# Five blocks of the output projection moved into the last attention units, and the residual chains in another order

## The chip, the cores and the metric

The kernel runs on one core of a Trainium2 chip. TensorE (PE) does matmuls into PSUM, VectorE (DVE) and ScalarE (ACT) work on vectors, GpSimd (POOL) does little here, and SyncE (SP) issues most loads. The metric is the time of one execution on the device in microseconds; lower is better. 2829.44 us is the median of three runs of the kernel before.

## The reference

One transformer block on 1024 tokens of width 1024, with 256 context tokens, in fp32. A hybrid mixer (differential attention of 4 heads, and a short convolution of width 512) is projected by `w_out`; the result is normalised, gated and added to `x`; a router chooses 128 tokens for each of 16 experts.

```
out  = concat([attn, conv], -1) @ w_out            # the mixer's output projection
h    = x + G1 * rmsnorm(out)                        # G1: gate times gain, from the ada vector
xn2  = rmsnorm(h) * A2 + SH2                        # A2, SH2: scale and shift
aff  = softmax(xn2 @ w_router)                      # 16 experts
g, i = top_k(aff.T, 128)                            # for each expert its 128 tokens
y    = scatter(g * (silu(xn2[i] @ w_gate) * (xn2[i] @ w_up)) @ w_down)
```

## The kernel before

Each fp32 operand is split into a high part in fp32r (an ACT cast) and the rest (a DVE subtraction), and each product is three matmuls, hi*hi, hi*lo and lo*hi (`mm3`, with `split` at L87 and L88). A scheduler orders the instructions when the program is built; on the chip each engine works its own list in order, and so does each DMA queue.

**Attention** runs 32 units, four heads by eight blocks of 128 queries. A unit has its scores (`sc`, one unit ahead), the softmax (`probs`: the exponentials `e`, their sum and scaling on ACT and DVE, then ten transposes `tp` and their split into `a`), and, for every second unit, the products with V for two query blocks (`values`: 30 matmuls `av`, a norm, and a store of the columns to `mixT_d` in DRAM by POOL's queue). Between them the 18 convolution jobs, 24 matmuls each, are spread over the first `NCV` units. At the end of unit `NCV` - 1, `out_weights` loads w_out in eight pieces of 512 KB through two `raw` buffers and splits them into `woh` and `wol`, which stay in SBUF.

**Phase 2** then loads the rows `G1`, `SH2`, `A2` and the router weights `wr`, and sends `SH2` through the router once (`rb`). For each of eight token blocks, `mixed` loads the block's columns of `mixT_d` (`mraw`), splits them (`mh`, `ml`), and runs 2 x 24 matmuls `mm<-woh` and `mm<-wol` into two PSUM banks. Behind them stands the residual chain: squares on ACT (L608), `rstd`, two operations with `G1` on DVE (L613), the addition of `x` (L614), another square (L616), the product with `A2` (`xn`, L620), eight transposes of `xn` on PE (L640), their copies (L641), sixteen router matmuls `lg` (L644), and a softmax that ends with L631 on DVE. Two blocks together give 32 rows of `affT`. When all of `affT` is there, `choose` runs 16 rounds of MAX8 and its companions on DVE (L656 first), and the expert layers follow; the small `ple` projection stands on PE behind the last block's router matmuls. From the sixth block on, the loads of the first expert weights (`next_raw`) stand between the blocks.

## Time and profile before

| | |
|---|---|
| median of 3 runs | 2829.44 us (2826.55 to 2829.99) |
| the profiled execution | 2830.79 us, its span 2828.9 us |
| mean granted clock of TensorE | 0.97 |
| busy share of the span | PE 93%, DVE 71%, ACT 57%, POOL 9% |

The profile is of one execution; the span runs from its first instruction to its last, and the execution's own time is 1.9 us longer. Attention's last part, phase 2 and the start of the top-k rounds lie between 280 and 700 us of the span; the rest of the program is the projection before and the experts behind, which the change does not touch.

### The profile page before, as it was taken

How to read it: one execution, taken by the hardware profiler on the slowest of the kernel's cores; microseconds unless marked ns; L12 is line 12 of the kernel's file. 1: busy time of each engine (PE TensorE's matmuls, PEld its weight loads, DVE VectorE, ACT ScalarE, POOL GpSimd, SP SyncE). 2: the span in 40 equal slices, each digit the busy share in tenths (PEclk: the TensorE clock that was granted, in tenths of full speed). 3: DMA queues.
4: the chain of work that ended last, by engine and by line, in shares of the span. 5: the costliest groups of instructions: out<-in, count | busy, mean ns of one | idle time of the engine just before them, and what ended most of it. 6: DMA issues, size and time to landing. Idle time of an engine off the chain costs nothing.

```text
span 2828.9 us, 38725 instructions
## 1 busy us (share of the span) xinstructions
PE 2636.2 (93%) x14237; PEld 2216.2 (78%) x14237; DVE 1998.8 (71%) x3298; ACT 1620.6 (57%) x2858; POOL 250.1 (9%) x355
## 2 busy tenths in 40 slices
PE   8999999898799999997799999998999998989998
PEld 5777888787588877775689999997878787777786
DVE  6965899845698888885656767763777676785535
ACT  4213898734477777775644555543665665674335
POOL 0101000001300000000100000000111110231000
PEclk9999999999899999999799999999999999999999
DMA  7666332245699999997512122336665667465612
GB/s 302 203 236 211 90 96 90 91 160 198 241 390 381 363 377 370 375 359 239 218 39 46 46 46 38 49 79 171 168 168 136 161 156 144 143 186 200 195 60 82
DMA packets 306018, 516.44 MB, mean 183 GB/s; under 512 B 52529, under 2 KB 180094, under 8 KB 304804
## 3 DMA queue, kind: packets, MB, share of 16 engines
q1 hardware_dynamic: 288556, 456.04, 51.0%
q0 software_dynamic: 11136, 36.25, 4.3%
q10 hardware_dynamic: 6136, 21.67, 2.0%
q8 instruction: 113, 1.85, 0.3%
q14 instruction: 77, 0.63, 0.1%
HBM read 421.01 MB, written 92.88 MB: 182 GB/s over the span
## 4 chain that ended last, share of the span: by engine, by line
PE 72%; DMA 10%; ACT 7%; DVE 6%; issue 3%; SPq 1%; POOL 0%; DVEq 0%; ACTq 0%; POOLq 0%
PE mm L82 13%; PE mm L84 13%; PE mm L83 12%; PE av L1333 2%; PE pu L763 2%; PE pu L764 2%; PE pu L762 2%; PE pg L763 2%; PE py L764 2%; PE py L763 2%; PE py L762 2%; PE pg L764 2%; PE sc L1052 2%; PE pg L762 2%; PE tp L1324 1%
## 5 line engine op out<-in xcount | busy, mean ns | idle before, releaser
L88 DVE TENSOR_TENSOR wlo<-raw,whi 128x2048 fp32r<-128x2048 f32 (+1 forms) x280 | 541.9, 1962 | 172.2 <-ACT whi L87 168.1
L87 ACT CAST whi<-raw 128x2048 fp32r<-128x2048 f32 (+1 forms) x284 | 459.8, 1656 | 136.5 <-PE mm L83 62.1
L82 PE MATMUL mm<-uh,whi 128*128 128x512 f32 x640 | 257.4, 402 | 0.9 <-ACT uh L824 0.9
L83 PE MATMUL mm<-ul,whi 128*128 128x512 f32 x640 | 254.1, 397 | 0.0
L84 PE MATMUL mm<-uh,wlo 128*128 128x512 f32 x640 | 253.8, 397 | 0.0
L84 PE MATMUL mm<-whi,ul 128*128 128x256 f32 x768 | 220.9, 288 | 0.0
L82 PE MATMUL mm<-whi,uh 128*128 128x256 f32 x768 | 220.6, 287 | 0.0
L83 PE MATMUL mm<-wlo,uh 128*128 128x256 f32 x768 | 218.2, 284 | 0.0
L82 PEld LDWEIGHTS mm<-whi,uh 128*128 128x128 f32 x768 | 147.4, 192 | 0.2
L84 PEld LDWEIGHTS mm<-whi,ul 128*128 128x128 f32 x768 | 147.5, 192 | 0.1
L83 PEld LDWEIGHTS mm<-wlo,uh 128*128 128x128 f32 x768 | 147.2, 192 | 0.2
L1302 ACT ACTIVATE lg<-lg,sm 128x128 f32<-128x128 f32 (+7 forms) x128 | 99.5, 777 | 82.2 <-DVE sm L1301 81.6
L84 PEld LDWEIGHTS mm<-uh,wlo 128*128 128x128 f32 x640 | 122.3, 191 | 24.4
L446 ACT ACTIVATE e<-sc,mx 128x512 f32<-128x512 f32 (+1 forms) x192 | 117.9, 624 | 40.3 <-DVE mx L445 39.5
L82 PEld LDWEIGHTS mm<-uh,whi 128*128 128x128 f32 x640 | 122.2, 191 | 22.9 <-ACT uh L824 1.4
L83 PEld LDWEIGHTS mm<-ul,whi 128*128 128x128 f32 x640 | 122.4, 191 | 21.7
L82 PE MATMUL mm<-xh,whi 128*128 128x512 f32 x320 | 127.2, 399 | 2.4 <-DVE stl L88 1.4
L1333 PE MATMUL av<-pT,V 128*128 128x256 f32 x640 | 109.9, 300 | 19.6 <-ACT pT L87 13.8
L83 PE MATMUL mm<-xl,whi 128*128 128x512 f32 x320 | 126.9, 398 | 0.0
L84 PE MATMUL mm<-xh,wlo 128*128 128x512 f32 x320 | 126.3, 396 | 0.5 <-DVE wlo L88 0.5
L1333 PEld LDWEIGHTS av<-pT,V 128*128 128x128 f32 x640 | 92.3, 196 | 43.0 <-ACT pT L87 30.5
L1298 DVE SCALAR_TENSOR_TENSOR lg<-sc,FT,nF 128x512 f32<-128x512 f32 (+3 forms) x160 | 91.6, 582 | 39.7 <-PE sc L1295 27.1
(392 smaller groups left out, 7006.2 us busy)
## 6 DMA issues: line engine op xcount, KB each, us to landing
raw<-in_w_gate_dram SPq DMA_DIRECT2D x64, 1024.0 KB
raw<-in_w_up_dram SPq DMA_DIRECT2D x64, 1024.0 KB
raw<-in_w_down_dram SPq DMA_DIRECT2D x64, 1024.0 KB
raw<-in_w_in_dram SPq DMA_DIRECT2D x76, 512.0 KB
wada<-in_w_ada_dram SPq DMA_DIRECT2D x32, 512.0 KB
Q<-Q_d SPq DMA_DIRECT2D x64, 256.0 KB
yraw<-yT_d SPq DMA_DIRECT2D x22, 512.0 KB
wa<-in_w_ada_dram SPq DMA_DIRECT2D x8, 1024.0 KB
```

The lines of the kernel that those rows point to most:

```text
L82: self.nc.tensor.matmul(ps, ah, bh, start=(i == 0), stop=False)
L83: self.nc.tensor.matmul(ps, ah, bl, start=False, stop=False)
L84: self.nc.tensor.matmul(ps, al, bh, start=False, stop=(i == n - 1))
L87: self.nc.scalar.copy(hi, src)
L88: (eng or self.nc.vector).tensor_tensor(lo, src, f(hi), op=ALU.subtract)
L446: nc.scalar.activation(e[:, c0:c0 + n], ps[:, :n], AF.Exp, scale=-1.0, bias=mx[:, m, c:c + 1], accum_out=sm[:, m, c:c + 1])
L762: self.nc.tensor.matmul(ps[n], xh[:, i, :], hi[:, k, c], start=(i == 0), stop=False)
L763: self.nc.tensor.matmul(ps[n], xh[:, i, :], lo[:, k, c], start=False, stop=False)
L764: self.nc.tensor.matmul(ps[n], xl[:, i, :], hi[:, k, c], start=False, stop=(i == KB - 1))
L1298: nc.vector.scalar_tensor_tensor(lg[:, c0:c0 + full], ps[:, :full], Ft, nF[:, c0:c0 + full], op0=ALU.subtract, op1=ALU.add)
L1302: nc.scalar.activation(lg[:, :n], lg[:, :n], AF.Exp, scale=-1.0, bias=sm[:, 0:1], accum_out=sm[:, 1:2])
L1333: nc.tensor.matmul(ps[:, :256], V[:, k, :], pT[k // 4][j][:, k % 4, :], start=(k + j == 0), stop=(k == nkb - 1 and j == 1))
```

## The change

`NCV` falls from 31 to 27, so that the convolution ends and w_out is loaded four units sooner. In the units 28 to 31, ahead of `probs`, `out_early` does the whole output projection of token blocks 0 to 3, and behind the last `probs` that of block 4. It loads the block's columns of `mixT_d`, splits them, runs the two halves through one PSUM bank (`mm`, one buffer), copies each to SBUF (`cy`) on ACT, and stores the block to the new DRAM tensor `pre_d` on POOL's queue. Phase 2 loads `pre_d` back into three of the six buffers of the weight loads, and its blocks go in the order out(5), chain 0, chain 4, out(6), chain 1, chain 5, out(7), chains 2, 6, 3, 7, where only blocks 5, 6 and 7 have matmuls. `rb` is computed behind the matmuls of block 5.

```diff
--- before.py
+++ after.py
@@ -30,7 +30,8 @@
 CAP = 128
 SB = 1
 LOOK = 1
-NCV = 31
+NCV = 27
+EARLY = 5
 NR = 6
 PB = 4
 FPROJ = 104
@@ -81,7 +82,7 @@
         for i, ((ah, al), (bh, bl)) in enumerate(pairs):
             self.nc.tensor.matmul(ps, ah, bh, start=(i == 0), stop=False)
             self.nc.tensor.matmul(ps, ah, bl, start=False, stop=False)
-            self.nc.tensor.matmul(ps, al, bh, start=False, stop=(i == n - 1))
+            self.lastmm = self.nc.tensor.matmul(ps, al, bh, start=False, stop=(i == n - 1))
 
     def split(self, src, hi, lo, eng=None):
         self.nc.scalar.copy(hi, src)
@@ -116,6 +117,7 @@
         self.dr = self.pool(st, "dram", space=DRAM)
         dt = lambda n, s, d=F32: self.t(self.dr, s, d, n)
         self.mixT_d = dt("mixT_d", [D, SEQ])
+        self.pre_d = dt("pre_d", [EARLY * P, D])
         self.h_d = dt("h_d", [SEQ, D])
         self.K_d = dt("K_d", [HEADS, 2, P, KEYS])
         self.Q_d = dt("Q_d", [HEADS, 2, P, SEQ])
@@ -393,7 +395,11 @@
                 self.conv(*x, w, 1)
             if i + 1 == NCV:
                 self.out_weights(w)
+            if 0 <= i - n + EARLY - 1 < EARLY - 1:
+                self.out_early(i - n + EARLY - 1, w)
             self.probs(i, *E.pop(i))
+            if i + 1 == n:
+                self.out_early(EARLY - 1, w)
             if i % 2:
                 self.values(i)
 
@@ -411,6 +417,30 @@
                     r0 = kh * 512 + j * 256
                     nc.sync.dma_start(raw, self.I["w_out"][0, r0:r0 + 256, n * 512:(n + 1) * 512].rearrange("(k p) c -> p k c", p=P))
                     self.split(raw, hi[:, j * 2:j * 2 + 2, :], lo[:, j * 2:j * 2 + 2, :])
+
+    def out_early(self, tb, w):
+
+        nc = self.nc
+        part = self.out_lhs(w, tb, ("raw", "whi", "wlo"), (2, 2))
+        y = self.t(w, [P, SEQ], F32, "cy", bufs=1)
+        for n in range(2):
+            ps = self.t(self.pp, [P, 512], F32, "mm", bufs=1)
+            self.out_half(ps, part, n)
+            nc.scalar.copy(y[:, n * 512:(n + 1) * 512], ps)
+        self.store(self.pre_d[tb * P:(tb + 1) * P, :], y)
+
+    def out_lhs(self, w, tb, tags, bufs):
+        raw = self.t(w, [P, KB, P], F32, tags[0], bufs=bufs[0])
+        self.nc.sync.dma_start(raw, self.mixT_d[:, tb * P:(tb + 1) * P].rearrange("(k p) t -> p k t", p=P))
+        mh = self.t(w, [P, KB, P], F32R, tags[1], bufs=bufs[1])
+        ml = self.t(w, [P, KB, P], F32R, tags[2], bufs=bufs[1])
+        self.split(raw, mh, ml)
+        return mh, ml
+
+    def out_half(self, ps, part, n):
+        mh, ml = part
+        wo = self.wo
+        self.mm3(ps, [((mh[:, k, :], ml[:, k, :]), (wo[n, k // 4][0][:, k % 4, :], wo[n, k // 4][1][:, k % 4, :])) for k in range(KB)])
 
     def scores(self, i):
         nc, w, pp = self.nc, self.wp, self.pp
@@ -547,15 +577,19 @@
         with ExitStack() as st:
             w = self.pool(st, "p2")
             pp = self.pool(st, "p2p", 2, space=PSUM)
-            wo = self.wo
             G1, SH2, A2 = [self.t(w, [P, D], F32, f"row{i}") for i in range(3)]
             for i, r in enumerate((G1, SH2, A2, self.G2)):
                 nc.sync.dma_start(r, rowbc(self.row_d[i:i + 1, :]))
             wr = self.t(w, [P, KB, NE], F32, "wr")
             nc.sync.dma_start(wr, I["w_router"][0].rearrange("(k p) e -> p k e", p=P))
             affT = self.t(w, [2 * NE, 512], F32, "affT")
-            self.rb = self.t(w, [P, 64], F32, "rb")[:, :NE]
-            nc.scalar.copy(self.rb, self.routed(w, pp, SH2, wr)[:, :NE])
+            self.rb = self.t(w, [P, P], F32, "rb")[:, :NE]
+            pre = []
+            for b in range(0, EARLY, 2):
+                raw = self.t(self.rawp, [P, 2, D], F32, "raw")
+                for j in range(min(2, EARLY - b)):
+                    nc.sync.dma_start(raw[:, j, :], self.pre_d[(b + j) * P:(b + j + 1) * P, :])
+                    pre.append(raw[:, j, :])
             self.raws = []
             self.wblocks = []
             for e in range(NE + 1):
@@ -563,20 +597,33 @@
                     self.wblocks += [(n, e, q) for n in ("w_gate", "w_up") for q in range(4)]
                 if e:
                     self.wblocks += [("w_down", e - 1, q) for q in range(4)]
-            for i in range(8):
+            af, pss, i = {}, {}, 0
+            for tb in (5, 0, 4, 6, 1, 5, 7, 2, 6, 3, 7):
+                if tb >= EARLY and tb not in pss:
+                    part = self.out_lhs(w, tb, ("mraw", "mh", "ml"), (1, 2))
+                    pss[tb] = [self.t(pp, [P, 512], F32, "mm", bufs=4) for n in range(2)]
+                    for n in range(2):
+                        self.out_half(pss[tb][n], part, n)
+                    continue
+                if i == 0:
+                    with self.tc.issue_after(self.lastmm.ins):
+                        nc.scalar.copy(self.rb, self.routed(w, pp, SH2, wr)[:, :NE])
                 if i == 4:
                     ple = self.ple_load(w)
                 if i >= 5:
                     self.next_raw(self.gate)
                     self.next_raw(self.gate)
-                if i % 2 == 0:
-                    af = self.t(w, [P, 2, NE], F32, "af", bufs=2)
-                self.mixed(w, pp, (i % 2) * 4 + i // 2, wo, G1, SH2, A2, wr, af[:, i % 2, :])
-                self.lastaf = af[0:1, i % 2, 0:1]
-                if i % 2:
+                i += 1
+                q, half = tb % 4, tb // 4
+                if q not in af:
+                    af[q] = self.t(w, [P, 2, NE], F32, "af", bufs=4)
+                src = pss[tb] if tb >= EARLY else [pre[tb][:, n * 512:(n + 1) * 512] for n in range(2)]
+                self.mixed(w, pp, tb, src, G1, SH2, A2, wr, af[q][:, half, :])
+                self.lastaf = af[q][0:1, half, 0:1]
+                if half:
                     tp = self.t(pp, [P, 512], F32, "lg")
-                    nc.tensor.transpose(tp[:2 * NE, :P], af.rearrange("p a e -> p (a e)"), self.ident)
-                    self.lastT = nc.vector.tensor_copy(affT[:, (i // 2) * P:(i // 2 + 1) * P], tp[:2 * NE, :P])
+                    nc.tensor.transpose(tp[:2 * NE, :P], af[q].rearrange("p a e -> p (a e)"), self.ident)
+                    self.lastT = nc.vector.tensor_copy(affT[:, q * P:(q + 1) * P], tp[:2 * NE, :P])
             self.stx.close()
             self.mw = self.pool(self.stx, "mw", 4, side="right")
             self.nb = 0
@@ -589,24 +636,16 @@
             n, e, q = self.wblocks[i]
             self.raws.append(self.rawrows(self.I[n][0, e, q * 256:(q + 1) * 256, :], after))
 
-    def mixed(self, w, pp, tb, wo, G1, SH2, A2, wr, af):
+    def mixed(self, w, pp, tb, pss, G1, SH2, A2, wr, af):
+
         nc, I = self.nc, self.I
         t = slice(tb * P, (tb + 1) * P)
-        raw = self.t(w, [P, KB, P], F32, "mraw", bufs=1)
-        nc.sync.dma_start(raw, self.mixT_d[:, t].rearrange("(k p) t -> p k t", p=P))
-        mh = self.t(w, [P, KB, P], F32R, "mh", bufs=2)
-        ml = self.t(w, [P, KB, P], F32R, "ml", bufs=2)
-        self.split(raw, mh, ml)
         x = self.t(w, [P, D], F32, "x", bufs=2)
         nc.sync.dma_start(x, I["x"][0, t, :])
         s2 = self.t(w, [P, 4], F32, "s2", bufs=2)
         tmp = self.t(w, [P, D], F32, "tmp", bufs=1)
-        pss = []
         for n in range(2):
-            ps = self.t(pp, [P, 512], F32, "mm", bufs=4)
-            self.mm3(ps, [((mh[:, k, :], ml[:, k, :]), (wo[n, k // 4][0][:, k % 4, :], wo[n, k // 4][1][:, k % 4, :])) for k in range(KB)])
-            nc.scalar.activation(tmp[:, n * 512:(n + 1) * 512], ps, AF.Square, accum_out=s2[:, n:n + 1])
-            pss.append(ps)
+            nc.scalar.activation(tmp[:, n * 512:(n + 1) * 512], pss[n], AF.Square, accum_out=s2[:, n:n + 1])
         nc.vector.tensor_tensor(s2[:, 2:3], s2[:, 0:1], s2[:, 1:2], op=ALU.add)
         self.rstd(s2[:, 2:3], D)
         for n in range(2):
```

TensorE where attention ends, before: the last of the products with V (`av`), the sums of squares for the norm (`ones`), the transposes and router matmuls of `rb`, then the first matmuls with w_out.

```order
L84 MATMUL av_5603<-a_1061_5546,V_880_4620 128x256
L487 MATMUL av_5638<-osq_5635,ones_63 128x256
L640 MATMUL tp_5674<-ident_59,row_1081_5663 128x128 x4
L640 MATMUL tp_5680<-ident_59,row_1081_5663 128x128 x4
L644 MATMUL lg_5686<-wr_5669,xT_5673 128x16 x8
L82 MATMUL mm_5707<-woh_5489,mh_5699 128x512
L83 MATMUL mm_5707<-wol_5490,mh_5699 128x512
L82 MATMUL mm_5733<-woh_5509,mh_5699 128x512
L83 MATMUL mm_5733<-wol_5510,mh_5699 128x512
```

After, on TensorE, the first matmul with w_out (`mm_5354`, block 0; `whi` is the block's high part) stands between the scores (`sc`) of the next units; no convolution matmul stands in the 95 rows ahead of it.

```order
L85 MATMUL av_5272<-a_982_5169,V_886_4679 128x256
L474 MATMUL sc_5455<-K_4672,Q_992_5195 128x512
L83 MATMUL mm_5354<-woh_5112,whi_5349 128x512
L84 MATMUL mm_5354<-wol_5113,whi_5349 128x512
L473 MATMUL sc_5460<-K_4672,Q_991_5194 128x256
L474 MATMUL sc_5460<-K_4672,Q_992_5195 128x256
L517 MATMUL av_5307<-osq_5304,ones_63 128x256
L473 MATMUL sc_5466<-K_4673,Q_993_5196 128x512
L85 MATMUL mm_5354<-woh_5112,wlo_5350 128x512
L83 MATMUL mm_5354<-woh_5112,whi_5349 128x512
```

The first w_out matmul moved from behind the whole of attention to a place ahead of the last four units' scores, transposes and products with V.

SP's queue at the start of phase 2, before: the last of the eight w_out pieces, the rows, the router weights, then the first blocks' `mraw` and `x`.

```order
L412 DMA raw_5525<-in_w_out_dram 128x2x512
L553 DMA row_1080_5662<-row_d_81 128x1024
L553 DMA row_1081_5663<-row_d_81 128x1024
L553 DMA row_1082_5664<-row_d_81 128x1024
L553 DMA G_1078_5651<-row_d_81 128x1024
L555 DMA wr_5669<-in_w_router_dram 128x8x16
L596 DMA mraw_5697<-mixT_d_76 128x8x128
L601 DMA x_5703<-in_x_dram 128x1024
L601 DMA x_5808<-in_x_dram 128x1024
L1347 DMA raw_6124<-in_w_ple_dram 128x2x1024
L596 DMA mraw_5802<-mixT_d_76 128x8x128
```

SP's queue at the same place after: the last two of five early loads of `mixT_d` (`raw`), the rows, the router weights, then the loads of `pre_d`, and behind them the `mraw` of block 5.

```order
L434 DMA raw_5750<-mixT_d_76 128x8x128
L434 DMA raw_5844<-mixT_d_76 128x8x128
L582 DMA row_1111_5963<-row_d_82 128x1024
L582 DMA row_1112_5964<-row_d_82 128x1024
L582 DMA row_1113_5965<-row_d_82 128x1024
L582 DMA G_1109_5952<-row_d_82 128x1024
L584 DMA wr_5970<-in_w_router_dram 128x8x16
L591 DMA raw_5974<-pre_d_77 128x1024 x2
L591 DMA raw_5977<-pre_d_77 128x1024 x2
L591 DMA raw_5980<-pre_d_77 128x1024
L434 DMA mraw_5982<-mixT_d_76 128x8x128
L644 DMA x_6062<-in_x_dram 128x1024
L644 DMA x_6111<-in_x_dram 128x1024
```

Five loads of `pre_d` now stand between `wr` and the first `mraw`; the last of them reads what the store of block 4 writes.

TensorE at the end of phase 2, before: the last two matmuls of block 7's output, then that block's transposes and router matmuls and the first transposes of ple (`px`).

```order
L83 MATMUL mm_6504<-wol_5520,mh_6470 128x512
L84 MATMUL mm_6504<-woh_5519,ml_6471 128x512
L640 MATMUL tp_6543<-ident_59,xn_6540 128x128 x4
L640 MATMUL tp_6549<-ident_59,xn_6540 128x128 x4
L644 MATMUL lg_6555<-wr_5669,xT_6542 128x16 x4
L1362 MATMUL tp_6582<-ident_59,px_6580 128x128 x2
L644 MATMUL lg_6555<-wr_5669,xT_6542 128x16 x4
```

After, the last matmuls of block 7's output (`mm_6328`), and then the transposes and router matmuls of the blocks 2, 6 and 3 (and of 7 behind them), and the pair's transposition of `af`.

```order
L83 MATMUL mm_6328<-woh_5142,mh_6323 128x512
L84 MATMUL mm_6328<-wol_5143,mh_6323 128x512
L85 MATMUL mm_6328<-woh_5142,ml_6324 128x512
L679 MATMUL tp_6403<-ident_59,xn_6400 128x128 x4
L679 MATMUL tp_6409<-ident_59,xn_6400 128x128 x4
L683 MATMUL lg_6415<-wr_5970,xT_6402 128x16 x8
L679 MATMUL tp_6458<-ident_59,xn_6455 128x128 x4
L679 MATMUL tp_6464<-ident_59,xn_6455 128x128 x4
L683 MATMUL lg_6470<-wr_5970,xT_6457 128x16 x8
L625 MATMUL lg_6488<-ident_59,af_6383 32x128
L679 MATMUL tp_6517<-ident_59,xn_6514 128x128 x4
L679 MATMUL tp_6523<-ident_59,xn_6514 128x128 x4
```

Where one block's transposes and router matmuls stood behind the last output matmul, now those of four blocks do; on DVE each block's first operation with `G1` stands behind the last softmax operation of the block before it, in both kernels.

## Rows read from the trace of the kernel before

**Rows 1.** The page of the profile, parts 1 and 4: TensorE's busy time, its share of the span and its instructions; and the chain of work that ended last, by engine.

```profile
PE 2636.2 (93%) x14237; PEld 2216.2 (78%) x14237; DVE 1998.8 (71%) x3298; ACT 1620.6 (57%) x2858; POOL 250.1 (9%) x355
...
PE 72%; DMA 10%; ACT 7%; DVE 6%; issue 3%; SPq 1%; POOL 0%; DVEq 0%; ACTq 0%; POOLq 0%
```

**Rows 2.** The table by stretch: stretch, its length, busy microseconds of each engine with the instructions in brackets, then the granted TensorE clock (1.00 is full), the DMA engines' share and GB/s.

```profile
280.00:540.00 260.00, 256.48 (x1504) 216.25 (x1502) 235.73 (x580) 226.27 (x613) 9.44 (x21) 1.00 0.27 80
542.00:562.00 20.00, 12.00 (x57) 9.88 (x56) 14.00 (x27) 13.58 (x23) 0.54 (x1) 0.66 0.59 204
...
572.00:578.00 6.00, 6.00 (x16) 4.61 (x16) 2.73 (x2) 1.90 (x1) 0.00 (x0) 0.53 0.63 199
580.00:680.00 100.00, 99.91 (x525) 84.41 (x524) 51.80 (x85) 39.37 (x105) 3.73 (x6) 1.00 0.52 177
682.00:691.00 9.00, 3.46 (x16) 3.27 (x17) 4.78 (x6) 3.72 (x10) 0.00 (x0) 0.77 0.63 254
691.00:699.00 8.00, 8.00 (x31) 6.80 (x32) 1.76 (x7) 3.40 (x9) 1.62 (x3) 0.62 0.28 98
```

**Rows 3.** The timeline of TensorE at the end of attention: start, length, line and operation, and in brackets how long the engine had been idle and what ended it. `mm<-xl,whi` belongs to the convolution, `tp` are transposes of the probabilities, `av` the products with V.

```profile
534.84 0.39 PE L83 MATMUL mm<-xl,whi 128*128 128x512 f32 x1
535.07 0.39 PE L84 MATMUL mm<-xh,wlo 128*128 128x512 f32 x1
...
536.17 1.29 PE L472 MATMUL tp<-ident,e 128*128 128x128 f32 x8
...
542.18 0.28 PE L83 MATMUL av<-a,V 128*128 128x256 f32 x1
542.30 0.28 PE L84 MATMUL av<-a,V 128*128 128x256 f32 x1
...
546.90 1.08 PE L472 MATMUL tp<-ident,e 128*128 128x128 f32 x4 [2.78 <-DVE e L465]
549.32 1.59 PE L472 MATMUL tp<-ident,e 128*128 128x128 f32 x6 [1.34 <-DVE e L465]
553.28 1.12 PE L472 MATMUL tp<-ident,e 128*128 128x128 f32 x4 [2.37 <-DVE a L88]
...
555.45 1.48 PE L472 MATMUL tp<-ident,e 128*128 128x128 f32 x6
...
561.77 0.28 PE L84 MATMUL av<-a,V 128*128 128x256 f32 x1
```

**Rows 4.** The split of w_out, from the timelines of SP's queue and of DVE (the first and the last of the eight subtractions), and, from the groups by line between 260 and 540 us, ACT's copy of one PSUM bank of 128x512.

```profile
539.66 15.16 SPq L412 DMA_DIRECT2D raw<-in_w_out_dram  x6
...
538.40 1.23 DVE L88 TENSOR_TENSOR wol<-raw,woh 128x1024 fp32r<-128x1024 f32 x1
...
561.99 1.22 DVE L88 TENSOR_TENSOR wol<-raw,woh 128x1024 fp32r<-128x1024 f32 x1 [2.32 <-ACT woh L87]
...
L516 ACT COPY cu<-mm 128x512 f32<-128x512 f32 x6 | 3.5, 583 | 1.2 <-PE mm L84 1.2
```

**Rows 5.** The timeline of TensorE at the start of phase 2: the transposes and router matmuls of `rb`, and the first output projection matmuls.

```profile
564.04 1.09 PE L640 MATMUL tp<-ident,row 128*128 128x128 f32 x8 [0.45 <-DMA row<-row_d]
567.05 3.26 PE L644 MATMUL lg<-wr,xT 128*128 128x16 f32 x16 [1.92 <-DMA wr<-in_w_router_dram]
571.52 0.79 PE L82 MATMUL mm<-woh,mh 128*128 128x512 f32 x1 [1.21 <-ACT mh L87]
...
577.65 0.40 PE L82 MATMUL mm<-woh,mh 128*128 128x512 f32 x1
```

**Rows 6.** The way of a mixer block through memory: SP's issue of the load of `mraw`, ACT's cast behind it, and from the DMA issues between 500 and 720 us the time to landing of POOL's 512 KB store from SBUF to DRAM (the last number of the row).

```profile
583.54 7.76 SPq L596 DMA_DIRECT2D mraw<-mixT_d  x2
...
587.43 1.06 ACT L87 CAST mh<-mraw 128x1024 fp32r<-128x1024 f32 x1 [0.38 <-DMA mraw<-mixT_d]
...
mixT_d<-cy POOLq DMA_DIRECT2D x1, 512.0 KB, 3.7
```

**Rows 7.** The residual chains: DVE's first operation on a block (L613) and its last (L631) for the blocks that start at 657.58, 670.97 and 683.47, then the first MAX8; from the chain that ended last, the transposes and the two groups of router matmuls of the block of 670.97; and TensorE's transposes of the last block.

```profile
657.58 1.41 DVE L613 SCALAR_TENSOR_TENSOR tmp<-mm,s,row 128x512 f32<-128x512 f32 x2 [0.60 <-ACT s L93]
...
668.17 0.23 DVE L631 TENSOR_SCALAR af<-af,r 128x16 f32<-128x16 f32 x1
...
670.97 1.39 DVE L613 SCALAR_TENSOR_TENSOR tmp<-mm,s,row 128x512 f32<-128x512 f32 x2
...
680.79 0.23 DVE L631 TENSOR_SCALAR af<-af,r 128x16 f32<-128x16 f32 x1
...
683.47 1.41 DVE L613 SCALAR_TENSOR_TENSOR tmp<-mm,s,row 128x512 f32<-128x512 f32 x2 [0.60 <-ACT s L93]
...
695.24 0.23 DVE L631 TENSOR_SCALAR af<-af,r 128x16 f32<-128x16 f32 x1
...
699.02 0.68 DVE L656 MAX8 vi<-affT 32x8 f32<-32x512 f32 x1
...
675.51 0.87 PE tp L640 x8
677.30 0.80 PE lg L644 x8
678.66 0.80 PE lg L644 x8
...
687.54 1.94 PE L640 MATMUL tp<-ident,xn 128*128 128x128 f32 x8 [5.66 <-DVE xn L620]
```

## The prediction

> **What bounds the kernel now.** I read the page first: TensorE is busy 93% of the span and holds 72% of the chain that ended last [rows 1], so it is the bound on average. The table by stretch then says where that is not so. From 280 to 540 us, in attention, PE works 256.5 of 260 us at clock 1.00; from 580 to 680 us, in the output projection, 99.9 of 100 [rows 2]. Between and behind them it starves: 12.0 of the 20 us from 542 to 562 at 0.66, and 3.5 of the 9 us from 682 to 691 at 0.77 [rows 2]. The first gap is the end of attention: the last convolution matmul is gone, and what is left of PE's work waits for DVE's `e` and `a` [rows 3]. The second is the last block's residual chain alone: PE waits 5.66 us for `xn` [rows 7].
>
> The end of this part of the program is the first MAX8 at 699.02 [rows 7], since the top-k rounds need the last block's `affT`, and ple and MoE stand in the same order behind it in both kernels. So the sum is the movement of that point, in three stretches: the end of av(31), the first `woh` matmul of phase 2, the first MAX8.
>
> **1. Attention up to the end of av(31): +51.7.** Five blocks of 48 matmuls move into it. A 128x512 matmul follows the one before by 0.228 us (534.84 to 535.07 [rows 3]), so 240 of them are 54.7 us, in a stretch where PE has no room before 540. That the 432 convolution matmuls go through 27 units rather than 31 costs nothing: PE is full either way.
>
> They do fill the gap. From 542.4 to the last av(31) matmul, which ends at 562.05, are 19.6 us. At full clock the work in it is 20 transposes at 0.16 (8 in 1.29), 30 av matmuls at 0.12 and 0.7 of ones, 7.6 us [rows 3]. So 12.0 us come back.
>
> Against that stands the split of w_out. Its eight loads, casts and subtractions took from 538.40 to the end of the last `wol` at 563.2, 24.8 us, through two raw buffers [rows 4]. Before, nothing waited for them until 571.52. After, the first matmul with `woh` stands in PE's queue behind about 16 us of attention work without convolution (60 av matmuls at 0.12, 22 transposes at 0.16, 28 matmuls of the scores at 0.12 or 0.228 by their width), and all that is queued behind it, scores of the next unit too, waits with it; DVE's softmax then waits for those scores. The wait is between 0 (the first half needs only four of the eight pieces) and 24.8 - 16 = 8.8. I take 6, nearer to the row, since DVE and ACT are still 91% and 87% busy there [rows 2].
>
> The ten halves share one PSUM buffer, so each waits for ACT's copy of the half before it: 0.58 us [rows 4] and some 0.1 of latency. Nothing to 7; transposes and av matmuls stand between most halves in PE's queue, so 3. ACT's ten copies (5.8 us) and the five splits (1.05 on ACT and 1.22 on DVE each) lie beside PE, which has 48 x 0.228 = 10.9 us of out matmuls for each block. Sum: 54.7 - 12.0 + 6 + 3 = 51.7, with bounds of 42.7 and 58.5.
>
> **2. End of av(31) to the first `woh` matmul of phase 2: -1.7.** Before: 571.52 - 562.05 = 9.5, for PE computed `rb` first and then waited for `mh` [rows 5]. Now `rb` comes later, but `mraw` of block 5 stands in SP's queue behind the last pre_d load, which waits for the store of block 4. That is ACT's copy 0.6, the store 3.7 to landing, the load 3.9 (issue at 583.54, cast at 587.43), cast 1.05 [rows 6], and 0.7 that I allow for the two issues, less the 18 av matmuls at 0.12 that PE still does: 7.8. If block 4's store meets a fuller queue, this is 3 more; without the store ahead of it 4 less.
>
> **3. First `woh` matmul to the first MAX8: -23.4.** Before: 699.02 - 571.52 = 127.5, at PE's pace of 48 matmuls and a chain per block. After, only three blocks have matmuls, and DVE's order keeps the eight chains apart: each block's first operation on `G1` stands behind the last softmax operation of the block before. So this stretch is a string of chains:
> - out(5): 48 x 0.228 = 10.9, and 2.9 since PE starts near half clock after its wait, as it did before (0.53 [rows 2]; the 14 matmuls from 571.52 to 577.65 took 6.1 us, where 0.228 each makes 3.2 [rows 5]): 13.8.
> - `rb`, now behind it on PE: before, 564.04 to 570.31 with 1.92 of waiting for `wr` [rows 5]: 4.4.
> - chain 0 from its transposes to its end: in the block of 670.97, from 674.9 (`xn` ready, 0.6 before its transposes at 675.51) to 681.02: 6.1 [rows 7].
> - seven chains more. With out matmuls beside them they took 10.8 (657.58 to 668.40) and 10.05 (670.97 to 681.02); the last, alone and at half clock, took 12.0 (683.47 to 695.47) [rows 7]. Three (4, 1, 5) at the mean of the first two: 31.2. Then PE has no out matmul left, and between the chains 2, 6, 3 little to do, as from 682 to 691: 11.0 each, half way between 10.05 and 12.0: 33.0. The last: 12.0.
> - from its end to MAX8, 3.6.
>
> Sum 13.8 + 4.4 + 6.1 + 76.2 + 3.6 = 104.1, so 23.4 less than 127.5. Bounds for one chain: 12.0 throughout (-15.6 for the stretch), and 8.5, the block of 670.97 without the 1.5 us that its transposes and router matmuls stood behind out matmuls (0.63 before the first, 0.34 behind the copy and 0.56 between the two groups [rows 7]): -40.1.
>
> The clock decides much of this. The row: PE's clock was 0.77 while the last chain ran with PE 38% busy and 0.62 behind it [rows 2], and eight transposes took 1.94 us instead of 0.87 [rows 7]. The Trainium skill, in TensorE: Matmul & The Clock Gate, under HAM oscillation, warns that a matmul stream broken by idle gaps keeps falling back to the half clock. By that, chains 2, 6 and 3 would cost 12.0 each (the sum 3 more); were PE kept at full clock, 10.05 or less (the sum 3 less). The rows decide between them only half, so I stay in the middle.
>
> **Sum.** 51.7 - 1.7 - 23.4 = +26.6 us. PE's 240 matmuls go into attention at full price, and what they leave behind is not PE's to shorten: a chain takes its 10 to 12 us whether or not PE has work beside it. The profiled execution took 2830.8, so 2857.4; it lies 1.4 above the median of the runs, so the forecast for the median is 2856.0.
>
> **Rivals.**
> - *Faster: the chains overlap.* DVE was busy 51.8 us in the 100 us from 580 to 680 [rows 2], in which 7.2 blocks passed: 7.2 a block, 6.0 without the split of `ml`. If chains ran at DVE's pace of 6.0, the stretch would be 27.9 + 42.0 = 69.9, and the sum 50.0 + 69.9 - 127.5 = -7.6: 2821.8. It decides from 7.1 us a chain downward. Against it: each engine's queue is in order, and the DVE rows stand one block behind the other. Chance 0.08.
> - *No change.* No stall at w_out and none at the PSUM buffer (42.7), and chains at 8.5: 42.7 - 1.7 - 40.1 = +0.9: 2830.3. For it: blocks 0 to 4 read SBUF and their squares can be done early. Against it: it needs three lower bounds at once. Chance 0.11.
> - *Much slower.* w_out exposed with 8.8, each half waiting for its copy with 7, chains at 12.0: 58.5 - 1.7 - 15.6 = +41.2: 2870.6. For it: DVE and ACT are nearly full when w_out arrives, and the last chains have nothing to hold the clock up. Chance 0.11.
>
> **How the numbers follow.** The forecast holds 0.70, with a range of its own from 2841 to 2867 (chains at 9.5 to 11.8, stalls of 3 to 15). 0.2% of this kernel is 5.7 us, about what a measurement of it can tell from no change. The range that leaves out 2 in 10 is 2831 to 2868. Faster by over 0.2%: 0.08 and a little of the forecast's own lower tail, 0.09. Within it: 0.11. Slower: 0.80.
>
> **What would show it.** PE's first `mm` with `woh` should start some 535 us into the span and wait for `wol`; av(31) should end near 614; the first `mh` matmul of phase 2 should come 7 to 8 us behind it, at half clock; and from the last out matmul on PE should be some 35% busy, with the chains 2, 6, 3 and 7 one behind the other at 10.5 to 12 us, and MAX8 near 725. The prediction is wrong if two blocks' `G1` operations stand less than 9 us apart there, or if PE in the units 28 to 31 waits for neither `wol` nor the copy.

## The result, and the profile after

The changed kernel takes 2855.73 us (median of four runs, 2850.77 to 2858.28) against 2827.99 of the kernel before beside it: a ratio of 1.0087, 95% interval 1.0066 to 1.0108. It is slower, as forecast, and the time is that of the forecast (2856.0). The profiled execution took 2858.3. From its page, the span and the busy times:

```profile
span 2856.4 us, 38764 instructions
...
PE 2649.7 (93%) x14237; PEld 2225.4 (78%) x14237; DVE 2000.3 (70%) x3298; ACT 1626.5 (57%) x2868; POOL 253.9 (9%) x360
```

PE's busy share is the 93% of before [rows 1]. Its instructions are as many as before (14237), but they were busy 13.5 us longer in a span that is 27.5 us longer; so about half of what was added is PE's work taking longer (mean granted clock 0.963 instead of 0.970), and the rest is waiting. The table by stretch of the changed kernel, with the columns of [rows 2]:

```profile
516.40:546.00 29.60, 22.08 (x113) 17.60 (x112) 26.61 (x49) 24.19 (x53) 1.08 (x2) 0.77 0.50 164
546.00:620.10 74.10, 73.19 (x365) 60.48 (x363) 28.85 (x66) 31.85 (x73) 3.76 (x7) 1.00 0.32 113
620.10:627.90 7.80, 0.71 (x3) 0.31 (x3) 2.02 (x5) 4.41 (x11) 0.55 (x1) 0.81 0.83 270
627.90:729.40 101.50, 79.95 (x385) 68.38 (x386) 54.12 (x94) 42.40 (x119) 5.52 (x9) 0.75 0.58 208
...
700.00:720.00 20.00, 8.74 (x39) 7.85 (x40) 11.18 (x22) 7.17 (x22) 1.30 (x2) 0.50 0.94 332
```

The stretches are: last convolution matmul to first `woh` matmul, from there to the end of av(31), the wait for block 5, first `mh` matmul to MAX8, and a part of the last chains. The corners of these on PE's timeline:

```profile
516.11 0.40 PE L85 MATMUL mm<-xh,wlo 128*128 128x512 f32 x1
...
545.97 0.40 PE L83 MATMUL mm<-woh,whi 128*128 128x512 f32 x1
...
619.79 0.28 PE L85 MATMUL av<-a,V 128*128 128x256 f32 x1
...
627.89 0.80 PE L83 MATMUL mm<-woh,mh 128*128 128x512 f32 x1 [6.29 <-ACT mh L88]
...
640.94 1.03 PE L679 MATMUL tp<-ident,row 128*128 128x128 f32 x8
...
718.04 1.94 PE L679 MATMUL tp<-ident,xn 128*128 128x128 f32 x8 [5.84 <-DVE xn L659]
```

Executions start attention up to 5 us apart, and the 2120 us of identical work behind MAX8 differ too (last section), so stages are compared from the start of each run's first scores (257.7 before, 259.0 after). The runs e1, e3, e5, e6 and e10 were executed once each (2861.46, 2847.89, 2856.98, 2860.28 and 2868.31 us), so their stages are read and not their totals. The table holds times in us, worked out from the timelines:

| kernel | last conv. matmul to first `woh` | first scores to end of av(31) | to first `mh` matmul | to MAX8 | first scores to MAX8 |
|---|---|---|---|---|---|
| before | | 304.4 | 9.5 | 127.5 | 441.3 |
| after | 29.9 | 361.1 | 7.8 | 101.5 | 470.4 |
| e1_no_wol | 28.9 | 360.5 | 7.8 | 101.0 | 469.3 |
| e2_own_buffer | 28.7 | 360.3 | 7.8 | 100.8 | 468.9 |
| e3_before_ncv27 | | 315.7 | 6.3 | 126.8 | 448.8 |
| e4_early2 | 26.2 | 333.2 | 7.4 | 113.3 | 453.9 |
| e5_two_pieces | 24.5 | 355.5 | 7.9 | 101.0 | 464.4 |
| e6_look2 | 28.3 | 362.3 | 7.4 | 99.8 | 469.5 |
| e7_overlap | 29.6 | 360.8 | 8.1 | 93.5 | 462.3 |
| e8_warm | 28.9 | 360.1 | 7.8 | 94.7 | 462.7 |
| e9_early0 | | 304.5 | 7.1 | 130.0 | 441.6 |
| e10_load_first | 29.2 | 360.4 | 3.5 | 113.0 | 476.9 |
| e11_early2_overlap | 26.9 | 334.2 | 7.4 | 108.5 | 450.0 |
| e12_eight_two_po | | 303.1 | 3.5 | 136.1 | 442.6 |

So the change lengthened attention by 56.7, shortened the transition by 1.7 and phase 2 by 26.0: 29.1 at MAX8.

What PE waited for between 500 and 740 us (total, times, longest):

```profile
PE tp L679 <- DVE xn L659: 17.3, 4, 5.8
PE mm L83 <- ACT mh L88: 6.3, 1, 6.3
PE tp L502 <- DVE e L495: 5.8, 3, 2.7
...
PE sc L473 <- ACT e L476: 2.0, 3, 0.9
...
PE mm L83 <- ACT cy L429: 0.7, 1, 0.7
```

The residual chains, one behind the other: the last softmax operation of each of the eight blocks in their order, and MAX8:

```profile
649.93 0.24 DVE L670 TENSOR_SCALAR af<-af,r 128x16 f32<-128x16 f32 x1
...
656.07 0.23 DVE L670 TENSOR_SCALAR af<-af,r 128x16 f32<-128x16 f32 x1
...
668.92 0.23 DVE L670 TENSOR_SCALAR af<-af,r 128x16 f32<-128x16 f32 x1
...
680.08 0.23 DVE L670 TENSOR_SCALAR af<-af,r 128x16 f32<-128x16 f32 x1
...
691.38 0.23 DVE L670 TENSOR_SCALAR af<-af,r 128x16 f32<-128x16 f32 x1
...
702.36 0.23 DVE L670 TENSOR_SCALAR af<-af,r 128x16 f32<-128x16 f32 x1
...
713.75 0.23 DVE L670 TENSOR_SCALAR af<-af,r 128x16 f32<-128x16 f32 x1
...
725.73 0.23 DVE L670 TENSOR_SCALAR af<-af,r 128x16 f32<-128x16 f32 x1
...
729.40 0.68 DVE L695 MAX8 vi<-affT 32x8 f32<-32x512 f32 x1
```

Behind the first two, each block ends 11.0 to 12.9 us after the one before. The second, block 4, ended 6.1 us behind block 0: its operations with `G1` ran long before block 0's softmax ended at 649.93, so DVE's order does not stand one block behind the other here.

```profile
638.00 1.41 DVE L652 SCALAR_TENSOR_TENSOR tmp<-raw,s,row 128x512 f32<-128x512 f32 x2
```

The queue in front of block 5's `mraw`: POOL's store of block 4, then SP's five loads of `pre_d`, which hold the queue for 34 us:

```profile
618.83 0.53 POOL L77 DMA_DIRECT2D pre_d<-cy  x1 [12.35 <-ACT cy L429]
...
587.61 34.42 SPq L591 DMA_DIRECT2D raw<-pre_d  x5
622.08 0.43 SPq L434 DMA_DIRECT2D mraw<-mixT_d  x1
```

### The profile page after: what moved, and what is told of

The parts are those of the page before. It is cut to its first block, busy times and chain, and to the rows that moved or that the text cites. A ratio compares the mean times of both kernels' runs of the same rounds, so it can differ in the third digit from the quotient of the medians.

```text
span 2856.4 us, 38764 instructions
## 1 busy us (share of the span) xinstructions
PE 2649.7 (93%) x14237; PEld 2225.4 (78%) x14237; DVE 2000.3 (70%) x3298; ACT 1626.5 (57%) x2868; POOL 253.9 (9%) x360
## 4 chain that ended last, share of the span: by engine, by line
PE 68%; DMA 11%; DVE 7%; ACT 7%; issue 5%; POOL 1%; SPq 0%; DVEq 0%; ACTq 0%; POOLq 0%
PE mm L83 12%; PE mm L85 12%; PE mm L84 12%; PE av L1372 2%; PE pu L802 2%; PE pu L803 2%; PE pu L801 2%; PE pg L802 2%; PE py L803 2%; PE py L802 2%; PE py L801 2%; PE pg L803 2%; PE sc L1091 2%; PE pg L801 2%; DMA Q_d<-stl 2%
## 5 line engine op out<-in xcount | busy, mean ns | idle before, releaser
L89 DVE TENSOR_TENSOR wlo<-raw,whi 128x2048 fp32r<-128x2048 f32 (+1 forms) x285 | 548.0, 1949 | 183.2 <-ACT whi L88 179.0
L83 PE MATMUL mm<-uh,whi 128*128 128x512 f32 x640 | 257.7, 403 | 0.9 <-ACT uh L863 0.9
L1372 PEld LDWEIGHTS av<-pT,V 128*128 128x128 f32 x640 | 93.5, 199 | 38.1 <-ACT pT L88 26.9
L475 DVE TENSOR_REDUCE mx<-sc 128x1 f32<-128x512 f32 (+1 forms) x192 | 109.2, 594 | 16.8 <-PE sc L474 15.8
```

What stands on the lines that cost most here:

```text
L83: self.nc.tensor.matmul(ps, ah, bh, start=(i == 0), stop=False)
L89: (eng or self.nc.vector).tensor_tensor(lo, src, f(hi), op=ALU.subtract)
L475: nc.vector.tensor_reduce(mx[:, m, c:c + 1], ps[:, :n], axis=AX.X, op=ALU.min)
L1372: nc.tensor.matmul(ps[:, :256], V[:, k, :], pT[k // 4][j][:, k % 4, :], start=(k + j == 0), stop=(k == nkb - 1 and j == 1))
```

## The experiments

**Whose is the stretch ahead of the first `woh` matmul?** It holds some 16 us of PE's work at full clock and took 29.9. Of the other 13.9 PE was idle 7.5 (29.60 less 22.08 in the table by stretch); the rest is longer matmuls at a granted clock of 0.77. Without the subtractions of w_out:

```diff
-                self.wo[n, kh] = hi, lo = [self.t(self.wop, [P, 4, 512], F32R, x) for x in ("woh", "wol")]
+                hi = self.t(self.wop, [P, 4, 512], F32R, "woh")
+                self.wo[n, kh] = hi, hi
...
-                    self.split(raw, hi[:, j * 2:j * 2 + 2, :], lo[:, j * 2:j * 2 + 2, :])
+                    nc.scalar.copy(hi[:, j * 2:j * 2 + 2, :], raw)
```

> The changed kernel without the eight subtractions of w_out: its low part is left out, and the matmuls with it take the high part, so this kernel computes the output projection with a coarser w_out. All matmuls stay. In the changed kernel 29.6 us pass from the end of the last convolution matmul (516.4) to the first matmul with woh (546.0), for 16 us of work. If DVE's queue sets that stretch (it was busy 26.6 of the 29.6), taking 8 x 1.22 = 9.8 us from it makes the stretch 6 to 10 us shorter, and the run about 2848. If what sets it is the loads of w_out through two raw buffers and ACT's casts, it is at most 2 us shorter, and the run stays within 3 us of 2856.

The stretch by the table of this run:

```profile
513.60:542.10 28.50, 19.50 (x108) 16.06 (x107) 17.03 (x37) 24.18 (x50) 1.08 (x2) 0.76 0.53 171
```

DVE is down from 26.6 to 17.0 us busy, and the stretch is one microsecond shorter. DVE's queue alone does not set it. (The total, 2861.46 us, lies outside the 3 us around 2856; av(31) and MAX8 do not move by more than 1.2.) With the early loads in a buffer of their own:

```diff
-        part = self.out_lhs(w, tb, ("raw", "whi", "wlo"), (2, 2))
+        part = self.out_lhs(w, tb, ("cu", "whi", "wlo"), (1, 2))
...
```

> The changed kernel with the five early loads of mixT_d in the buffer cu, which the convolution no longer needs, instead of the two raw buffers in which the pieces of w_out are. The load of block 0 then goes out before the last pieces of w_out are split (SP issued it at 540.1 in the changed kernel, after the last release). If that load is what the first matmul with woh waits for, it comes 3 to 5 us sooner, and the run is at 2851 to 2853. If PE's queue of attention work ahead of it is what counts, nothing changes (2854 to 2858).

28.7 instead of 29.9, 2858.21 us, ratio to before 1.0103 (1.0079 to 1.0126): no gain; the load was not waited for. With two of the eight pieces:

```diff
+                if n or kh:
+                    self.wo[n, kh] = self.wo[0, 0]
+                    continue
```

> The changed kernel with two of the eight pieces of w_out loaded, cast and subtracted; the other six are left out, and their matmuls take the first two, so the output projection is not that of the reference. All matmuls stay. The changed kernel needs 29.9 us from the start of the last convolution matmul to the start of the first with woh. If the split of w_out as a whole (loads, ACT's casts of 8.4 us, DVE's 9.8) makes that stretch longer than PE's 16 us, it comes down to 18 to 23 us here, and av(31) and MAX8 come 7 to 12 us sooner. If attention without convolution takes that long by itself, the chain from scores through the softmax to the transposes being what PE waits for, it stays at 27 or more.

```profile
514.30:538.40 24.10, 20.37 (x112) 16.85 (x111) 21.24 (x48) 19.87 (x50) 1.08 (x2) 0.79 0.22 72
```

24.5: six of the eight pieces of w_out are worth 5.4 us, nearly the 6 that I had taken for all, but 24.5 is still 8.5 more than PE's work. The first outcome expected is missed by 1.5 (and MAX8 comes 6.0 sooner where 7 to 12 stood), and the second did not come either. As leaving out the subtractions alone (e1) gave 1.0, most of the 5.4 seems to belong to the loads and ACT's casts; these were not left out by themselves. With the scores two units ahead (`LOOK = 2`):

> The changed kernel with the scores two units ahead instead of one (LOOK = 2). If PE's 13.9 us of lost time between the convolution and the first woh matmul come from the length of one unit's chain (scores, softmax, transposes), a second unit in flight shortens the stretch of 29.9 us by 5 us or more. If DVE and ACT are the bound there (26.6 and 24.2 us busy in 29.6), it stays within 3 us.

```profile
517.20:545.10 27.90, 20.21 (x89) 14.95 (x87) 24.38 (x42) 22.15 (x51) 1.08 (x2) 0.73 0.52 169
```

28.3: a second unit in flight takes 1.6 away, so one unit's length is not it either, though only 89 of PE's instructions fell into this stretch instead of 113, which makes it a weak witness. Last, the kernel before with nothing but `NCV = 27`:

> The kernel before with NCV = 27 alone: the convolution and w_out four units sooner, no output projection in attention, the old order of blocks. My theory: attention without convolution runs at the pace of DVE (some 49 us of work after the last convolution matmul in the changed kernel, without its splits of blocks), so av(31) ends 8 to 12 us later than the 562.1 of before, and the run is at 2834 to 2842. Then the 240 matmuls of the change cost 48 to 50 us on top, nearly their full 54.7. Rival: attention's tail has the same DVE and ACT work as before, PE's gaps only move, and the time does not change (2826 to 2832); then all of the 58 us that attention grew by belong to the moved matmuls and their waits.

Its first 29.6 us behind the convolution, and the whole tail:

```profile
518.90:548.50 29.60, 23.09 (x116) 18.22 (x115) 26.68 (x52) 24.58 (x56) 1.08 (x2) 0.77 0.37 129
518.90:577.00 58.10, 45.22 (x235) 35.49 (x233) 48.08 (x109) 45.45 (x109) 2.17 (x4) 0.82 0.33 110
```

The first row is that of the changed kernel without a moved matmul in it: in the same 29.6 us PE gets through 116 instructions, where the changed kernel had 113, and DVE and ACT are busy 26.7 and 24.6, where it had 26.6 and 24.2. Attention whose convolution has run out takes this long with the split of w_out alone beside it, and av(31) ends 11.3 us later (8 to 12 expected; at MAX8 it is 7.5). The run's total, 2847.9, lies above the 2842 expected, by the part behind MAX8 (2135.9 us against 2129.9). From this kernel to the changed one av(31) moves by another 45.4, which is 9.1 for each moved block.

**How many blocks?**

```diff
-NCV = 27
-EARLY = 5
+NCV = 30
+EARLY = 2
...
-            for tb in (5, 0, 4, 6, 1, 5, 7, 2, 6, 3, 7):
+            for tb in (4, 0, 5, 4, 2, 1, 6, 5, 3, 2, 7, 6, 3, 7):
```

> The changed kernel with two blocks moved instead of five (EARLY = 2, NCV = 30), and the order out 4, chain 0, out 5, chain 4, out 2, chain 1, out 6, chain 5, out 3, chain 2, out 7, chains 6, 3, 7. My theory: each block costs attention 10.9 us at full price, three blocks fewer give back 33 us of the 58, and phase 2 stays near 101 to 110 us from the first mh matmul to MAX8, since the string of chains sets it up to there (PE has 65 us of out matmuls and 19 of the chains in it). So MAX8 at 695 to 708 and the run at 2822 to 2837. Rival: PE's matmuls cost the same wherever they stand, and what the change lost is a fixed price for the w_out stretch and the new order; then the run stays at 2848 or more.

2841.31 us, ratio 1.0050 (1.0034 to 1.0066): between the two, and my figures are missed (2837 at most for the time, 110 for phase 2). Three blocks fewer give back 27.9 us of attention (9.3 each), and phase 2 takes back 11.8 (3.9 each):

```profile
598.90:712.20 113.30, 103.15 (x529) 87.37 (x530) 57.74 (x96) 46.05 (x122) 3.66 (x9) 0.89 0.57 201
```

The rival's fixed price is there (28.8 for two blocks is 10.2 more than two times 9.3), and I had left it out here; the matmuls' price is there as well. Each of the blocks three to five costs attention more than twice what it saves in phase 2.

**The order alone**, all blocks in phase 2 (`EARLY = 0`, `NCV = 31`, `rb` behind block 0's matmuls):

> The order part of the change alone: no block is moved (EARLY = 0, NCV = 31, w_out in the last units as before), but phase 2 is that of the changed kernel: rb behind the first block's matmuls, each block's output matmuls one or two chains ahead of its chain, no pre_d. My theory: PE has 88 us of out matmuls and 19 of the chains here and sets the pace, as before, so the stretch from the first mh matmul to MAX8 stays within 4 us of the 127.5 of before, and the run at 2825 to 2836; the loss of the change is then wholly in the moved matmuls. Rival: the new order itself costs (rb on PE's path, chains later), and the run is at 2840 or more.

2830.23 us, ratio 1.0010 (0.9999 to 1.0022). Phase 2 is 2.5 longer and the transition 2.4 shorter. With all blocks in phase 2 the order costs nothing, so the loss comes with the move: the matmuls themselves, and the convolution that makes room for them (e3).

**Is it the string of chains?** Each chain cut in two:

```diff
-        lg = self.routed(w, pp, xn, wr)
+        return lambda: self.mixed_end(w, pp, t, xn, s2, SH2, wr, af)
...
+                if ends is not None:
+                    self.finish(pp, af, affT, *ends)
+                ends = nxt
...
```

Here `finish` does the part from the transposes to the softmax of the block before.

> The changed kernel with the residual chains cut in two: a block's part up to xn stands ahead of the part from the transposes to the softmax of the block before it, with three buffers for x and two for tmp (and one instead of two for mh and ml, to make room). If the string of chains, one at a time, sets the 101.5 us from the first mh matmul to MAX8, they overlap now by some 2 us each or more, and this stretch falls to 83 to 92 us, the run to 2838 to 2848. If PE or the loads of x set it, it stays at 99 or more, and the run at 2853 or more.

93.5 instead of 101.5, and the run at 2843.38, ratio 1.0060 (1.0034 to 1.0085). The ends of the last six blocks on DVE:

```profile
676.46 0.23 DVE L681 TENSOR_SCALAR af<-af,r 128x16 f32<-128x16 f32 x1
...
690.17 0.23 DVE L681 TENSOR_SCALAR af<-af,r 128x16 f32<-128x16 f32 x1
...
697.54 0.23 DVE L681 TENSOR_SCALAR af<-af,r 128x16 f32<-128x16 f32 x1
...
704.70 0.23 DVE L681 TENSOR_SCALAR af<-af,r 128x16 f32<-128x16 f32 x1
...
712.65 0.23 DVE L681 TENSOR_SCALAR af<-af,r 128x16 f32<-128x16 f32 x1
...
718.99 0.23 DVE L681 TENSOR_SCALAR af<-af,r 128x16 f32<-128x16 f32 x1
```

The last four follow in 6.3 to 8.0 us instead of 11 to 12: the string sets this stretch, and chains that overlap shorten it. The whole is 1.5 short of what I expected: block 4 ends 15.2 us behind block 0 instead of 6.1, and 13.7 us pass between blocks 1 and 5. The single buffer for `mh` and `ml` has a part in it, since ACT stood idle for 5.3 us before its cast of block 7 into it, until block 6's matmuls were done; two buffers were not tried. With the clock held up:

```diff
-        lg = self.routed(w, pp, xn, wr)
+        lg = self.routed(w, pp, xn, wr, (x, G1) if tb in (2, 6, 3, 7) else None)
...
+        if warm:
+            tp = self.t(pp, [P, 512], F32, "tp")
+            for k in range(1):
+                nc.tensor.matmul(tp, warm[0][:, k * P:(k + 1) * P], warm[1][:, :512], start=True, stop=True)
...
+        if warm:
+            tp = self.t(pp, [P, 512], F32, "tp")
+            for k in range(4):
+                nc.tensor.matmul(tp, xT[:, k, :], warm[1][:, :512], start=True, stop=True)
```

> The changed kernel with matmuls added that nobody reads, for the blocks 2, 6, 3 and 7: one of 128x512 in fp32 behind x, ahead of the block's transposes, and four behind its router matmuls. They only keep PE busy between the chains. In the changed kernel the last four chains take 11.0 to 12.0 us each and PE's clock is 0.50 from 700 to 720. If the half clock is part of that length, the clock there rises to 0.9 or more and a chain falls to 9.0 to 10.2, so that MAX8 comes 5 to 9 us sooner and the run is at 2847 to 2852. If it is DVE's and ACT's operations and the latency between the engines, the clock rises and the chains stay at 10.7 or more (2853 to 2859), or the added matmuls stand in the way (above 2859).

The table by stretch, the first added matmul, and the ends of blocks 5, 2, 6, 3 and 7 on DVE with MAX8:

```profile
626.10:720.90 94.80, 82.27 (x408) 60.61 (x408) 54.42 (x94) 41.77 (x116) 3.70 (x8) 0.95 0.61 220
700.00:720.00 20.00, 15.39 (x71) 9.08 (x71) 11.33 (x20) 9.02 (x23) 1.47 (x3) 1.00 0.84 323
...
682.03 1.02 PE L679 MATMUL tp<-row,x 128*128 128x512 f32 x2
...
675.29 0.23 DVE L670 TENSOR_SCALAR af<-af,r 128x16 f32<-128x16 f32 x1
...
688.31 0.23 DVE L670 TENSOR_SCALAR af<-af,r 128x16 f32<-128x16 f32 x1
...
698.06 0.23 DVE L670 TENSOR_SCALAR af<-af,r 128x16 f32<-128x16 f32 x1
...
708.82 0.23 DVE L670 TENSOR_SCALAR af<-af,r 128x16 f32<-128x16 f32 x1
...
718.57 0.23 DVE L670 TENSOR_SCALAR af<-af,r 128x16 f32<-128x16 f32 x1
...
720.87 0.68 DVE L703 MAX8 vi<-affT 32x8 f32<-32x512 f32 x1
```

PE's clock from 700 to 720 is 1.00 instead of 0.50, and the last three chains take 9.8, 10.8 and 9.8 us instead of 11.0, 11.4 and 12.0, though block 2 took 13.0 instead of 11.3, with the first of the added matmuls beside it. So the half clock is part of a chain's length, as the first theory has it, even if one of the three chains stays above the 10.2 expected.

Phase 2 is 6.8 shorter, but only 3.8 of that lie behind the end of block 5. Up to there this execution was already 3.0 ahead (49.4 us behind the first `mh` matmul instead of 52.4), before the first added matmul ran. Two of these come in block 1's chain (10.9 us instead of 12.9), where the granted clock was 0.93 instead of 0.74 with the same instructions; the cause of that is open. The time is 2850.66 us, ratio 1.0080 (1.0057 to 1.0103), in the range of the first theory, but the interval overlaps that of the changed kernel (1.0066 to 1.0108): the gain is read from the stages.

**Where the string stops.** Two blocks moved, with overlapping chains:

> Two blocks moved, as in the fourth run, with the overlapping chains of the seventh. In the fourth run 113.3 us passed from the first mh matmul to MAX8, of which PE was busy 103. If PE's matmuls set that stretch again with six blocks in it, the overlap gives little: 106 to 112 us, the run at 2834 to 2841. If the string of chains still set it, it falls by the 8 us of the seventh run or more, to 105 or less, and the run to 2833 or less.

```profile
599.70:708.20 108.50, 103.71 (x527) 87.65 (x528) 55.99 (x96) 46.05 (x121) 2.54 (x9) 0.90 0.59 209
```

108.5 instead of 113.3, 2835.93 us, ratio 1.0022 (1.0008 to 1.0037), as the first outcome has it. PE is busy 103.7 of it, at a granted clock of 0.90: with six blocks in phase 2, PE is the bound again.

**The transition.**

```diff
+            part5 = self.out_lhs(w, 5, ("mraw", "mh", "ml"), (1, 2))
             G1, SH2, A2 = [self.t(w, [P, D], F32, f"row{i}") for i in range(3)]
...
-                    part = self.out_lhs(w, tb, ("mraw", "mh", "ml"), (1, 2))
+                    part = part5 if tb == 5 else self.out_lhs(w, tb, ("mraw", "mh", "ml"), (1, 2))
```

> The changed kernel with block 5's load of mixT_d and its split ahead of the rows and of pre_d in SP's queue; it needs nothing of the last unit. By step 2 of the prediction the first mh matmul stands 7.8 us behind av(31) because the load waits in the queue for the store of block 4: it should now come within 1 to 3 us. The string of chains is not shorter by that: chain 0 still needs pre_d, and the scheduler puts block 6's 48 matmuls ahead of chain 4's transposes, so I expect MAX8 from 5 us sooner to 5 us later. If the wait was for mixT_d itself (the store of the last unit) or for the cast, the 7.8 us stay.

The first `mh` matmul comes 3.5 us behind av(31) instead of 7.8, half a microsecond more than expected: the queue was the reason for 4.3 of the 7.8. Phase 2 grows by 11.5. Chain 0 is not sooner (it ends 27.6 us behind the first `mh` matmul instead of 22.3): behind the earlier load, SP's queue issued the rows only at 622.5, once attention's last unit was done, where the changed kernel had them at 583.4, and `pre_d` and `x` behind them, for which the chain waited. Block 4 ends 15.2 us behind it instead of 6.1, its transposes now behind block 6's matmuls. MAX8 comes 6.5 later, just outside what I expected. A gain ahead of a string of chains is lost if it lets PE start the wrong work.

**A version that beats both.**

```diff
-NCV = 27
-EARLY = 5
+NCV = 31
+EARLY = 0
...
+            part5 = self.out_lhs(w, 0, ("mraw", "mh", "ml"), (1, 2))
...
-            for tb in (5, 0, 4, 6, 1, 5, 7, 2, 6, 3, 7):
+            for tb in (0, 4, 0, 1, 4, 5, 1, 2, 5, 6, 2, 3, 6, 7, 3, 7):
...
-            o = self.t(w, [P, D], F32, "po", bufs=1)
+            o = self.t(w, [P, D], F32, "x", bufs=2)
```

> A try at a version that beats both: all eight blocks in phase 2 as in the ninth run, block 0's load ahead of the rows in SP's queue so that its matmuls follow av(31) directly, and two buffers instead of one for the output of ple (those of x, which is no longer needed there). In the kernel before, the transposes behind the top-k rounds start 4.9 us after DVE is done with them (739.94 to 735.04), since PE's queue has the ple matmuls ahead and these wait for the store of the single buffer. If both gains reach the end, 3 us from the transition and 2 to 5 from ple, the run is at 2821 to 2826; if the transition is taken back by rb and only one counts, at 2825 to 2829.

2821.80 us against 2828.23 (median of ten), ratio 0.9971 (0.9958 to 0.9984). In the kernel before, DVE's last operation on the top-k indices, PE's transposes of them, and the first expert matmul:

```profile
734.70 0.34 DVE L660 CAST vi<-idx 32x128 f32<-32x128 uint32 x1
...
739.94 0.31 PE L663 MATMUL tp<-ident,vi 32*128 32x32 f32 x2
...
749.65 0.80 PE L762 MATMUL pg<-whi,xsh 128*128 128x512 f32 x1 [1.07 <-ACT xsh L87]
```

and the same in this one:

```profile
736.86 0.21 DVE L698 CAST vi<-idx 32x128 f32<-32x128 uint32 x1
...
737.27 0.30 PE L701 MATMUL tp<-ident,vi 32*128 32x32 f32 x2
...
745.79 0.79 PE L800 MATMUL pg<-whi,xsh 128*128 128x512 f32 x1
```

The transposes follow DVE at once instead of 4.9 us later, and the first expert matmul comes 4.7 us sooner, counted from the first scores. The transition's 6.0 us are more than taken back in phase 2 (136.1 against 127.5; MAX8 comes 1.3 later), so only the gain at ple counts, though the time lies where I expected both. What the median gained beyond 4.7 us has not been traced, and the two edits were not run apart.

## Why the prediction was right

**Attention: +56.7 where +51.7 stood, and the term at fault is the w_out stall.** The 12.0 us that were to come back, since the moved matmuls fill PE's gap at the end, did come back there: from 546.0 to 620.1 PE was busy 73.2 of 74.1. But the gap went to the front. I had bounded the wait ahead of the first `woh` matmul by w_out's split, 8.8 at most; it was 13.9 (29.9 less 16), of which PE was idle 7.5 and ran the rest at a lower clock (0.77). Six of the eight pieces of the split are 5.4 of that (e5). The rest goes with attention without convolution: I had read off the end of before that PE starves there (12.0 of 20 us) and then not priced it for the units that the change empties (e3). What sets the pace of these units is not settled: taking work from DVE alone (e1) or putting a second unit in flight (e6) moved it little, and whether added matmuls, by holding the clock up, would shorten this stretch too was not tried. The PSUM copies cost 0.9 instead of 3: PE idled that much in the whole of the stretch, 0.7 of it for `cy`. With 13.9 and 0.9 in their places the sum is 54.7 - 12.0 + 13.9 + 0.9 = 57.5, against 56.7. That convolution in 27 units costs nothing holds while there is convolution: from 280 to 516 us PE was busy 234.1 of 236 at clock 1.00.

**Transition: -1.7, as worked out**, 7.8 us; e10 shows that the queue holds 4.3 of it. That it agrees to a tenth is luck in part: `mraw` was issued 3.25 us behind block 4's store (3.7 stood for the store), and ACT's cast began 4.7 behind that (3.9 stood, and 0.7 for two issues).

**Phase 2: -26.0 where -23.4 stood.** out(5) took 13.1 (13.8), `rb` and chain 0 9.2 (10.5), the chains of 4, 1 and 5 30.1 (31.2), of 2, 6 and 3 33.7 (33.0), the last 12.0 (12.0), and MAX8 followed 3.4 (3.6) later. The 30.1 are 6.1, 12.9 and 11.1: block 4 was under way beside block 0, against the order on DVE that the prediction and the text ahead of it state, and block 1 took longer. That these came near 31.2 together is luck. The clock of the last chains was 0.50, with PE idle 3.8 to 5.8 us ahead of their transposes, and with the clock held up the last three took 5.5 us less with what follows them up to MAX8 (e8). The Trainium skill (TensorE: Matmul & The Clock Gate, HAM oscillation) describes a kernel whose matmuls come in bursts broken by waits, each burst starting again at the lower clock; the trace agrees. On the price it lies in the middle: 33.7 for blocks 2, 6 and 3, where 12.0 each would be 36.0 and 10.05 each 30.2.

**The sum** was 26.6 and came out as 29.1 at MAX8: the two errors of 5.0 and 2.6 have opposite signs. The median moved by 27.7. That the time came within 0.3 us of the forecast is luck; that it lies in the range is not. Of the rivals, the overlapping of chains did not happen by itself but for block 4 (11 to 12.9 us from block to block behind it), and it has to be written into the kernel (e7). The sign that I named for a wrong prediction, that PE waits for neither `wol` nor the copy, is nearly there: it waited 0.7 for the copy and for `wol` not at all. The first `woh` matmul stood at 546.0 where 535 stood, av(31) ended at 620.1 (614) and MAX8 came at 729.4 (725). The time was right with one mechanism of it misread, the stall at w_out.

## What to carry to other kernels

Work that is moved into a stretch has to be priced against what that stretch was filled with: to make room, the filler goes elsewhere, and the stretch that it leaves shows the waits that it had hidden (here 24.5 to 29.9 us for 16 us of PE's work). Moving matmuls off a stretch helps only down to the chain that runs beside them; count the chain before the matmuls. And look at the queue behind the last step: in e12, with a second output buffer there and no block moved, the first expert matmul came 4.7 us sooner than in the kernel before, while the change cost 27.7 us.

## What the runs showed that was not expected

Matmuls that nobody reads can shorten a stretch: from the end of block 5 to MAX8 they made it 3.8 us shorter (e8), with the granted clock from 700 to 720 us up from 0.50 to 1.00. And from MAX8 to the end of the span, where all these kernels have the same work except for e12's two buffers, executions took from 2118.9 us (e7) to 2135.9 (e3); a single total says little about a change of 10 us here, while the stages ahead of MAX8 agree to 1.7 us wherever two kernels share them, but for the 3.0 us in e8 ahead of its first added matmul.
